# Attention scores of even and odd heads queued in pairs, in turn, in two PSUM banks

## The chip, the cores and the metric

The kernel runs on one core of one Trainium2 chip. The metric is the device time of one execution in microseconds. The engines are TensorE (PE in the rows; PEld is its weight loads), VectorE (DVE), ScalarE (ACT), GpSimd (POOL) and the DMA queues, which SyncE (SP) and others issue. Each engine works through its own queue in order and waits for others by semaphores.

## What is computed

Two transformer blocks over 256 tokens of width 1024, all in fp32: a gated MLP layer and a sliding-window attention layer, then a second block with a neighbourhood attention, a dilated attention and a product-key expert layer. Only the three attentions matter here. Cut to that:

```python
# sliding window (16 heads of 64, keys shared by 8 heads, sink per head)
scores = einsum('bnqhrd,bnkhd->bnhrqk', q, k_band) * 64 ** -0.5
scores = where(mask, scores, -inf)
m = maximum(max(scores), sink); p = exp(scores - m)
o = einsum('bnhrqk,bnkhd->bnqhrd', p / (sum(p) + exp(sink - m)), v_band)

# neighbourhood (8 heads) and dilated (8 heads): a bias or a mask per key, softmax over the keys
s = einsum('bhqd,bhqkd->bhqk', q, k[idx]) * 64 ** -0.5 + bias
o = einsum('bhqk,bhqkd->bhqd', softmax(s), v[idx])
```

The kernel computes each of them over all 256 keys (or 128 for the first token tile of the sliding window), with tables that add a large number where a key is out of reach.

## The kernel before, in words

Each projection is a product of three passes (`mm3`, lines 295 to 297): weights are split into a high and a low part, `hi` by ScalarE (L115, or L121 where the weights are scaled) and `lo` by VectorE or GpSimd (L116, L122), out of raw buffers that SyncE's DMA queue fills ahead. A projection goes in pieces: a unit of weights, its matmuls, then `tick()`. A tick runs what was deferred to it, and after that some units of a background list `bg`, as many as a rate says (3.0 in block B, 3.25 and 6.0 in block C). The scheduler is manual: every engine's queue has the order in which the program is written, and the ticks thus set where attention stands between the projections.

`attn` (L566) fills that list. Its work is cut into items. An item is one token tile of 128 queries and either four heads with 128 keys or two heads with 256 keys, and all heads of an item are even, or all are odd. A head has 64 dimensions; those of even heads lie in partitions 0 to 63 of `qT` and `kT`, or of `qkT`, and those of odd heads in 64 to 127. So the score products of an even item use one half of TensorE's rows, those of an odd item the other half. In the program's lists even and odd items alternate. An item has three units:

- S, `score(i)`: one PSUM tile `tr` (a bank) with the score products (L584); then for each head VectorE adds the bias and takes the minimum of the negated scores (L589, into `sc` and `nm`), and ScalarE takes the exponential with its sum (L592, into `pe`).
- T, `tr(i)`: four transposes of `pe` by TensorE (L608) into a `tr` tile, which ScalarE (L613, even items) or VectorE (L611, odd items) copies to `pT`.
- O, `ov(i)`: eight records of products of `pT` with v (L626) into the tile `o`. After the last item of eight heads `o_evac` follows on VectorE. In block C it divides (`yo`, L883), takes a sum of squares on ScalarE, a power on GpSimd (L212) and scales `yo` on VectorE (L888).

The order of the units was S(i), T(i-2), O(i-3), over and over. There are three `tr` banks. Others use them too: transposes of q (L696, copied by ScalarE at L697), of y and of other activations (L250, evacuated to `yThi` by ScalarE and to `yTlo` by VectorE, L252, L253, L258, L259), products for a bias table `nab` (L823, read by VectorE at L825) and two products for the modulation (`ada`, L451, read at L455). For the modulation VectorE also adds up `ada_acc` (L425) from weights that GpSimd's DMA queue loads.

Block B (sliding window) has 12 items. Block C has two times 8: the neighbourhood heads, here C0, and the dilated heads, here C1.

Of the kernel before, what the change touches and what calls it, by code (L numbers as in the profile page):

```python
# [37 lines left out]
P = 128  # L38
# [12 lines left out]
class Model:  # L51
# [514 lines left out]
    def attn(self, pool, items, qT, kT, v, bias, sink, osink, ready=lambda: True):  # L566


        nc = self.nc
        st = {}  # L570

        def score(i):
            tt, heads, kt = items[i]
            nk = len(kt) * P
            ps = self.tr_tile()
            pe = pool.tile([P, 512], F32, name="pe", tag="pe", bufs=3)
            key = "sum", tt, heads[0] // 8
            if key not in st:
                st[key] = pool.tile([P, 2, 8], F32, name="den", tag="den", bufs=3)
                st["min", key] = self.SM.tile([P, 8], F32, name="nm", tag="nm", bufs=3), []  # L580
            sm, (nm, seen) = st[key], st["min", key]
            for j, hd in enumerate(heads):
                js = slice(j * nk, (j + 1) * nk)
                nc.tensor.matmul(ps[:, js], qT(hd)[:, tt * P:(tt + 1) * P], kT(hd)[:, kt[0] * P:kt[0] * P + nk],  # L584
                                 start=True, stop=True)
            for j, hd in enumerate(heads):
                js = slice(j * nk, (j + 1) * nk)
                s = pool.tile([P, nk], F32, name="sc", tag="sc", bufs=4)
                nc.vector.tensor_tensor_reduce(s, ps[:, js], bias(hd, tt), scale=1.0,  # L589
                                               scalar=sink[:, hd:hd + 1] if sink is not None else BIG,  # L590
                                               op0=OP.add, op1=OP.min, accum_out=nm[:, hd % 8:hd % 8 + 1])
                nc.scalar.activation(pe[:, js], s, AF.Exp, scale=-1.0, bias=nm[:, hd % 8:hd % 8 + 1],  # L592
                                     accum_out=sm[:, 0, hd % 8:hd % 8 + 1])
                seen.append(hd)
            if sink is not None and len(seen) == 8:
                g0 = heads[0] // 8 * 8
                nc.vector.tensor_tensor(sm[:, 1], nm, sink[:, g0:g0 + 8], op=OP.subtract)
                nc.scalar.activation(sm[:, 1], sm[:, 1], AF.Exp)
            st[i] = pe

        def tr(i):
            tt, heads, kt = items[i]
            n = len(kt)
            ps = self.tr_tile()
            pe = st.pop(i)
            m = len(heads) * n
            for q in range(m):
                nc.tensor.transpose(ps[:, q * P:(q + 1) * P], pe[:, q * P:(q + 1) * P], self.ident)  # L608
            pT = pool.tile([P, 512], F32, name="pT", tag="pT", bufs=2)
            if i % 2:  # L610
                nc.vector.tensor_copy(pT[:, :m * P], ps[:, :m * P])  # L611
            else:
                nc.scalar.activation(pT[:, :m * P], ps[:, :m * P], AF.Copy)  # L613
            st[i] = pT

        def ov(i):
            tt, heads, kt = items[i]
            pT = st.pop(i)
            grp = heads[0] // 8
            if ("o", tt, grp) not in st:  # L620
                st["o", tt, grp] = self.o_tile()
            o = st["o", tt, grp]
            for j, hd in enumerate(heads):
                for q, kk in enumerate(kt):
                    c = j * len(kt) + q
                    nc.tensor.matmul(o[:, (hd % 8) * 64:(hd % 8 + 1) * 64], pT[:, c * P:(c + 1) * P], v(hd, kk),  # L626
                                     start=q == 0, stop=q == len(kt) - 1)
            if heads[-1] % 8 == 7:
                osink(tt, grp, st.pop(("o", tt, grp)), st.pop(("sum", tt, grp)))

        n = len(items)
        for i in range(n + 3):
            if i < n:
                self.bg.append(lambda i=i: score(i))
            if 0 <= i - 2 < n:
                self.bg.append(lambda i=i: tr(i - 2))
            if 0 <= i - 3 < n:
                self.bg.append(lambda i=i: ov(i - 3) if ready() else False)


    def block_b(self):
# [700 lines left out]
```

## Time and profile before

| | us |
|---|---|
| three runs | 1334.18, 1329.62, 1328.78 (median 1329.62) |
| the profiled execution | 1334.21 |
| its span, first to last instruction | 1332.5 |
| TensorE busy | 1292.4 (97%) |
| VectorE busy | 1006.7 (76%) |
| ScalarE busy | 643.7 (48%) |

A row of the views in order of time gives the start, the duration, the engine, the line, the operation, the tiles written and read, the shape and, in brackets, how long the engine had been idle before it and what ended that. Neighbours of one kind are merged (x8). TensorE's matmuls overlap in the pipeline, so a group's end and the next one's start lie over each other: what a group costs is read from its start to the next group's start. An fp32 product is two records. The granted clock (PEclk) is a share of 2.4 GHz, so 0.50 is 1.2 GHz.

### The profile page before, as it was taken

How to read it: one execution, taken by the hardware profiler on the slowest of the kernel's cores; microseconds unless marked ns; L12 is line 12 of the kernel's file. 1: busy time of each engine (PE TensorE's matmuls, PEld its weight loads, DVE VectorE, ACT ScalarE, POOL GpSimd, SP SyncE). 2: the span in 40 equal slices, each digit the busy share in tenths (PEclk: the TensorE clock that was granted, in tenths of full speed). 3: DMA queues.
4: the chain of work that ended last, by engine and by line, in shares of the span. 5: the costliest groups of instructions: out<-in, count | busy, mean ns of one | idle time of the engine just before them, and what ended most of it. 6: DMA issues, size and time to landing. Idle time of an engine off the chain costs nothing.

```text
span 1332.5 us, 21495 instructions
## 1 busy us (share of the span) xinstructions
PE 1292.4 (97%) x7898; PEld 1146.2 (86%) x7898; DVE 1006.7 (76%) x2086; ACT 643.7 (48%) x1125; POOL 158.5 (12%) x149
## 2 busy tenths in 40 slices
PE   8999999998999989999999999999999999999997
PEld 6888777786987869999999999999988888888886
DVE  5789777757756577979999999999765668666565
ACT  5555355663545335544544444444455555445544
POOL 1111112014102134730000000000000001000001
PEclk9999999998989989999999999999999999999999
DMA  7988787523765334555554444444457668655552
GB/s 275 336 266 278 235 267 217 141 80 126 258 232 182 118 122 151 172 170 169 180 168 162 140 143 143 143 143 143 159 188 238 224 213 272 205 192 190 194 196 100
DMA packets 85417, 250.90 MB, mean 188 GB/s; under 512 B 7776, under 2 KB 8944, under 8 KB 84672
## 3 DMA queue, kind: packets, MB, share of 16 engines
q1 hardware_dynamic: 74240, 208.17, 46.5%
q0 software_dynamic: 10208, 39.63, 9.3%
q10 hardware_dynamic: 864, 1.73, 0.3%
q8 instruction: 62, 1.02, 0.3%
q14 instruction: 43, 0.35, 0.1%
HBM read 247.40 MB, written 2.10 MB: 187 GB/s over the span
## 4 chain that ended last, share of the span: by engine, by line
PE 77%; DVE 11%; DMA 4%; issue 4%; ACT 2%; POOL 1%; POOLq 0%; ACTq 0%; DVEq 0%
PE mm L297 22%; PE mm L295 22%; PE mm L296 22%; PE tr L1092 4%; DVE lo L116 4%; DMA ada<-in_ada_w 2%; PE o L626 1%; PE tr L584 1%; DMA raw<-in_a_w_out 1%; DVE G L1047 1%; DVE G L1045 1%; PE tr L608 1%; POOL lo L116 1%; DMA ada<-in_norm_g 1%; ACT pe L592 1%
## 5 line engine op out<-in xcount | busy, mean ns | idle before, releaser
L116 DVE TENSOR_TENSOR lo<-raw,hi 128x1024 fp32r<-128x1024 f32 x340 | 416.5, 1229 | 131.7 <-ACT hi L115 129.3
L115 ACT ACTIVATE hi<-raw 128x1024 fp32r<-128x1024 f32 x376 | 394.5, 1052 | 182.7 <-PE mm L296 72.3
L295 PE MATMUL mm<-hThi,hi 128*128 128x256 f32 x1248 | 360.2, 289 | 0.0
L297 PE MATMUL mm<-hThi,lo 128*128 128x256 f32 x1248 | 354.3, 284 | 3.7 <-DVE lo L116 3.5
L296 PE MATMUL mm<-hTlo,hi 128*128 128x256 f32 x1248 | 353.3, 283 | 0.0
L297 PEld LDWEIGHTS mm<-hThi,lo 128*128 128x128 f32 x1248 | 239.4, 192 | 5.6 <-DVE lo L116 5.5
L295 PEld LDWEIGHTS mm<-hThi,hi 128*128 128x128 f32 x1248 | 239.7, 192 | 0.4 <-issue 0.3
L296 PEld LDWEIGHTS mm<-hTlo,hi 128*128 128x128 f32 x1248 | 239.9, 192 | 0.1
L296 PE MATMUL mm<-lo,whi 128*128 128x512 f32 x512 | 199.2, 389 | 0.0
L295 PE MATMUL mm<-hi,whi 128*128 128x512 f32 x512 | 199.2, 389 | 0.0
L297 PE MATMUL mm<-hi,wlo 128*128 128x512 f32 x512 | 199.2, 389 | 0.0
L1152 ACT ACTIVATE whi<-G 128x256 fp32r<-128x256 f32 x128 | 53.4, 418 | 167.1 <-PE mm L296 166.6
L295 PE MATMUL mm<-hi,hThi 128*128 128x512 f32 (+1 forms) x320 | 129.3, 404 | 0.7 <-ACT hThi L278 0.3
L296 PE MATMUL mm<-lo,hThi 128*128 128x512 f32 (+1 forms) x320 | 126.1, 394 | 0.5 <-DVE lo L116 0.5
L297 PE MATMUL mm<-hi,hTlo 128*128 128x512 f32 (+1 forms) x320 | 126.3, 395 | 0.2 <-DVE hTlo L279 0.2
L296 PEld LDWEIGHTS mm<-lo,whi 128*128 128x128 f32 x512 | 96.1, 188 | 20.1
L295 PEld LDWEIGHTS mm<-hi,whi 128*128 128x128 f32 x512 | 96.1, 188 | 20.1
L297 PEld LDWEIGHTS mm<-hi,wlo 128*128 128x128 f32 x512 | 96.1, 188 | 19.7
L1153 DVE TENSOR_TENSOR wlo<-G,whi 128x256 fp32r<-128x256 f32 x128 | 55.7, 436 | 62.2 <-ACT whi L1152 62.2
L116 POOL TENSOR_TENSOR lo<-raw,hi 128x1024 fp32r<-128x1024 f32 x36 | 89.1, 2480 | 104.8 <-ACT hi L115 104.8
L1084 DVE TENSOR_SCALAR ohg<-iota,slotT 128x128 f32<-128x128 f32 x256 | 87.4, 341 | 0.0
L1100 ACT ACTIVATE G<-tr 128x292 f32<-128x292 f32 (+31 forms) x64 | 19.7, 308 | 140.1 <-DVE G L1098 90.6
(239 smaller groups left out, 1627.4 us busy)
## 6 DMA issues: line engine op xcount, KB each, us to landing
raw<-in_u SPq DMA_DIRECT2D x128, 512.0 KB, 3.7
raw<-in_v SPq DMA_DIRECT2D x128, 512.0 KB, 4.4
raw<-in_a_w_in SPq DMA_DIRECT2D x48, 512.0 KB, 5.6
ada<-in_ada_w POOLq DMA_DIRECT2D x40, 512.0 KB, 4.9
raw<-in_w_in SPq DMA_DIRECT2D x24, 512.0 KB, 4.8
raw<-in_a_w_out SPq DMA_DIRECT2D x16, 512.0 KB, 5.9
raw<-in_b_w_in SPq DMA_DIRECT2D x16, 512.0 KB, 5.3
raw<-in_wq SPq DMA_DIRECT2D x12, 512.0 KB, 3.6
```

Of the source, the lines that this page charges most:

```text
L115: nc.scalar.activation(hi, raw, AF.Copy)
L116: e.tensor_tensor(lo, raw, hi.bitcast(F32), op=OP.subtract)
L295: nc.tensor.matmul(out, l[0], r[0], start=start, stop=False, skip_group_check=shared)
L296: nc.tensor.matmul(out, l[0], r[1], start=False, stop=False, skip_group_check=shared)
L297: nc.tensor.matmul(out, l[1], r[0], start=False, stop=stop, skip_group_check=shared)
L584: nc.tensor.matmul(ps[:, js], qT(hd)[:, tt * P:(tt + 1) * P], kT(hd)[:, kt[0] * P:kt[0] * P + nk], start=True, stop=True)
L592: nc.scalar.activation(pe[:, js], s, AF.Exp, scale=-1.0, bias=nm[:, hd % 8:hd % 8 + 1], accum_out=sm[:, 0, hd % 8:hd % 8 + 1])
L1084: nc.vector.tensor_scalar(og[:, j], self.iota, slotT[:, 0, t:t + 1], slotT[:, 2, t:t + 1], op0=OP.is_equal, op1=OP.mult)
L1092: nc.tensor.matmul(ps[:, j * P:(j + 1) * P], o[:, j], og[:, j], start=True, stop=True)
L1100: nc.scalar.activation(G[:, nb:, t0:t0 + 4], src[:, nb:], AF.Copy)
L1152: nc.scalar.activation(hi, G[:, b], AF.Copy)
L1153: nc.vector.tensor_tensor(lo, G[:, b], hi.bitcast(F32), op=OP.subtract)
```

## The change

The products of items i and i+1 (even and odd) are queued together when S(i) runs, with one tile each, head by head in turn; S(i+1) then has only its VectorE and ScalarE part. The list is built in pairs: S(i), T(i-2), S(i+1), T(i-1), O(i-2), O(i-1). The number of units is the same. All further lines move by 12 to 14.

```diff
--- before.py
+++ after.py
@@ -566,23 +566,35 @@
     def attn(self, pool, items, qT, kT, v, bias, sink, osink, ready=lambda: True):
 
 
+
         nc = self.nc
         st = {}
+
+        def products(i):
+            pair = (i, i + 1)
+            for q in pair:
+                st["ps", q] = self.tr_tile()
+            tt, heads, kt = items[i]
+            nk = len(kt) * P
+            assert items[i + 1][0] == tt and items[i + 1][2] == kt and len(items[i + 1][1]) == len(heads)
+            for j in range(len(heads)):
+                for q in pair:
+                    hd = items[q][1][j]
+                    nc.tensor.matmul(st["ps", q][:, j * nk:(j + 1) * nk], qT(hd)[:, tt * P:(tt + 1) * P],
+                                     kT(hd)[:, kt[0] * P:kt[0] * P + nk], start=True, stop=True)
 
         def score(i):
             tt, heads, kt = items[i]
             nk = len(kt) * P
-            ps = self.tr_tile()
+            if i % 2 == 0:
+                products(i)
+            ps = st.pop(("ps", i))
             pe = pool.tile([P, 512], F32, name="pe", tag="pe", bufs=3)
             key = "sum", tt, heads[0] // 8
             if key not in st:
                 st[key] = pool.tile([P, 2, 8], F32, name="den", tag="den", bufs=3)
                 st["min", key] = self.SM.tile([P, 8], F32, name="nm", tag="nm", bufs=3), []
             sm, (nm, seen) = st[key], st["min", key]
-            for j, hd in enumerate(heads):
-                js = slice(j * nk, (j + 1) * nk)
-                nc.tensor.matmul(ps[:, js], qT(hd)[:, tt * P:(tt + 1) * P], kT(hd)[:, kt[0] * P:kt[0] * P + nk],
-                                 start=True, stop=True)
             for j, hd in enumerate(heads):
                 js = slice(j * nk, (j + 1) * nk)
                 s = pool.tile([P, nk], F32, name="sc", tag="sc", bufs=4)
@@ -629,13 +641,15 @@
                 osink(tt, grp, st.pop(("o", tt, grp)), st.pop(("sum", tt, grp)))
 
         n = len(items)
-        for i in range(n + 3):
-            if i < n:
-                self.bg.append(lambda i=i: score(i))
-            if 0 <= i - 2 < n:
-                self.bg.append(lambda i=i: tr(i - 2))
-            if 0 <= i - 3 < n:
-                self.bg.append(lambda i=i: ov(i - 3) if ready() else False)
+        for i in range(0, n + 2, 2):
+            for j in (0, 1):
+                if i < n:
+                    self.bg.append(lambda i=i + j: score(i))
+                if i >= 2:
+                    self.bg.append(lambda i=i + j: tr(i - 2))
+            for j in (0, 1):
+                if i >= 2:
+                    self.bg.append(lambda i=i + j: ov(i - 2) if ready() else False)
 
 
     def block_b(self):
```

`products` takes two `tr` tiles at once. Which bank a tile gets is settled when the program is built: at the start of a stretch the second pair's odd tile gets the bank of the very first tile (in C0 tr_3229 that of tr_3206), and waits until VectorE's L589 steps on it are done. The first T after a pair's S takes the third bank. In C1's dense part the last T (into tr_3915) takes the bank of item 6 (tr_3888).

TensorE's queue at the start of C0, before; S are L584, T are L608, and tr_3206, tr_3218 and tr_3228 are the tiles of items 0 to 2, tr_3278 that of item 3:

```order
L584 MATMUL tr_3206<-qkT_2903 128x256 x2
L584 MATMUL tr_3218<-qkT_2903 128x256 x2
L584 MATMUL tr_3228<-qkT_2903 128x256 x2
...
L608 MATMUL tr_3271<-ident_92,pe_3207 128x128 x4
L584 MATMUL tr_3278<-qkT_2903 128x256 x2
L608 MATMUL tr_3288<-ident_92,pe_3219 128x128 x4
```

The same place now; S are L583, T are L620, and tr_3206, tr_3207, tr_3228, tr_3229 are the tiles of items 0 to 3:

```order
L583 MATMUL tr_3206<-qkT_2903 128x256
L583 MATMUL tr_3207<-qkT_2903 128x256
L583 MATMUL tr_3206<-qkT_2903 128x256
L583 MATMUL tr_3207<-qkT_2903 128x256
L583 MATMUL tr_3228<-qkT_2903 128x256
L583 MATMUL tr_3229<-qkT_2903 128x256
L583 MATMUL tr_3228<-qkT_2903 128x256
L583 MATMUL tr_3229<-qkT_2903 128x256
...
L620 MATMUL tr_3274<-ident_92,pe_3212 128x128 x4
L620 MATMUL tr_3288<-ident_92,pe_3221 128x128 x4
```

Left out are 24 projection matmuls. Item 3's products moved from behind them, and from behind the first T, to ahead of them.

TensorE's queue in C1's dense part, before; O are L626, and items 4 to 7 have their scores in tr_3830, tr_3853, tr_3874 and tr_3905:

```order
L626 MATMUL o_3825<-vs_2904,pT_3742 128x64 x4
L584 MATMUL tr_3830<-qkT_2903 128x256 x2
L608 MATMUL tr_3842<-ident_92,pe_3689 128x128 x4
L626 MATMUL o_3825<-vs_2904,pT_3759 128x64 x4
L584 MATMUL tr_3853<-qkT_2903 128x256 x2
L608 MATMUL tr_3863<-ident_92,pe_3745 128x128 x4
L626 MATMUL o_3825<-vs_2904,pT_3847 128x64 x4
L584 MATMUL tr_3874<-qkT_2903 128x256 x2
L608 MATMUL tr_3884<-ident_92,pe_3831 128x128 x4
L626 MATMUL o_3825<-vs_2904,pT_3868 128x64 x4
L584 MATMUL tr_3905<-qkT_2903 128x256 x2
L608 MATMUL tr_3915<-ident_92,pe_3854 128x128 x4
```

Now, the second half of it (the first half is the same with items 0, 1, 4, 5, 2 and 3); O are L638:

```order
L638 MATMUL o_3825<-vs_2904,pT_3854 128x64 x4
L638 MATMUL o_3825<-vs_2904,pT_3868 128x64 x4
L583 MATMUL tr_3888<-qkT_2903 128x256
L583 MATMUL tr_3889<-qkT_2903 128x256
L583 MATMUL tr_3888<-qkT_2903 128x256
L583 MATMUL tr_3889<-qkT_2903 128x256
L620 MATMUL tr_3901<-ident_92,pe_3840 128x128 x4
L620 MATMUL tr_3915<-ident_92,pe_3856 128x128 x4
```

Two O, two S and two T now follow each other, where O, S and T took turns. On VectorE, item 6's L589 stood ahead of the evacuation of `yo` before:

```order
L589 ISA sc_3878,nm_3833<-tr_3874,dib_2902 128x256
...
L589 ISA sc_3881,nm_3833<-tr_3874,dib_2902 128x256
...
L883 TENSOR_TENSOR yo_2907<-o_3825,den_3668 128x512
L888 TENSOR_SCALAR yo_2907<-yo_2907,rs_r_3902 128x512
```

Now it stands behind it (L601 was L589, L897 and L902 were L883 and L888):

```order
L897 TENSOR_TENSOR yo_2907<-o_3825,den_3673 128x512
L902 TENSOR_SCALAR yo_2907<-yo_2907,rs_r_3885 128x512
L601 ISA sc_3895,nm_3842<-tr_3888,dib_2902 128x256
...
L601 ISA sc_3898,nm_3842<-tr_3888,dib_2902 128x256
```

Since O(3) ends the first eight heads, and it is now written ahead of S(6), VectorE reads item 6's scores only after `yo` is scaled.

## Rows read from the trace of the kernel before

**Rows 1.** First part of the page: busy us, share of the span, instructions.

```profile
PE 1292.4 (97%) x7898; PEld 1146.2 (86%) x7898; DVE 1006.7 (76%) x2086; ACT 643.7 (48%) x1125; POOL 158.5 (12%) x149
```

**Rows 2.** TensorE in order of time (start, us, instruction), a lone S in C0.

```profile
386.45 1.00 PE L626 MATMUL o<-vs,pT 128*128 128x64 f32 x8
387.38 1.13 PE L584 MATMUL tr<-qkT 64*128 64x256 f32 x4
388.44 0.66 PE L608 MATMUL tr<-ident,pe 128*128 128x128 f32 x4
...
395.99 1.00 PE L626 MATMUL o<-vs,pT 128*128 128x64 f32 x8
396.81 0.36 PE L295 MATMUL mm<-hThi,hi 128*128 128x256 f32 x1
```

**Rows 3.** TensorE in order of time, the three S that open C0.

```profile
371.06 1.99 PE L584 MATMUL tr<-qkT 64*128 64x256 f32 x12
372.98 0.39 PE L295 MATMUL mm<-hThi,hi 128*128 128x256 f32 x1
```

**Rows 4.** TensorE and VectorE in order of time, the start of block B.

```profile
238.19 0.50 PE L295 MATMUL mm<-hi,hThi 128*128 128x512 f32 x1
238.43 0.08 DVE L589 DVE_READ_ACCUMULATOR2_ANT nm<- 128x1 f32 x1
```

**Rows 5.** ScalarE and TensorE in order of time, block B, the second T.

```profile
243.13 0.57 ACT L613 ACTIVATE pT<-tr 128x512 f32<-128x512 f32 x1
243.76 0.66 PE L608 MATMUL tr<-ident,pe 128*128 128x128 f32 x4 [0.20 <-ACT pT L613]
```

**Rows 6.** ScalarE, TensorE and VectorE in order of time, block B, transposes of q.

```profile
256.62 1.06 ACT L697 ACTIVATE qT<-tr 128x512 f32<-128x512 f32 x2
257.25 0.66 PE L608 MATMUL tr<-ident,pe 128*128 128x128 f32 x4 [0.41 <-ACT qT L697]
257.96 0.69 DVE L722 TENSOR_TENSOR q<-o,den 128x512 f32<-128x512 f32 x1
```

**Rows 7.** TensorE, VectorE and ScalarE in order of time, block B, transposes of y.

```profile
285.00 1.04 PE L250 MATMUL tr<-ident,q 128*128 128x128 f32 x8
285.20 0.69 DVE L825 TENSOR_TENSOR nab<-nam,tr 128x512 f32<-128x512 f32 x1 [1.31 <-PE tr L823]
285.64 1.09 ACT L252 ACTIVATE yThi<-tr 128x512 fp32r<-128x512 f32 x2 [0.67 <-PE tr L250]
286.27 1.29 DVE L253 TENSOR_TENSOR yTlo<-tr,yThi 128x512 fp32r<-128x512 f32 x2 [0.38 <-ACT yThi L252]
```

**Rows 8.** VectorE in order of time, the start of C0.

```profile
373.73 1.28 DVE L425 SCALAR_TENSOR_TENSOR ada_acc<-ada,silu_c,ada_acc 128x1024 f32<-128x1024 f32 x1 [7.41 <-DMA ada<-in_ada_w]
...
377.89 0.08 DVE L589 DVE_READ_ACCUMULATOR2_ANT nm<- 128x1 f32 x1
```

**Rows 9.** TensorE in order of time, the first T of C0.

```profile
378.31 1.18 PE L608 MATMUL tr<-ident,pe 128*128 128x128 f32 x4 [2.21 <-DVE nm L589]
```

**Rows 10.** Stretches: length, busy us of PE, PEld, DVE, ACT, POOL; PEclk, DMA share, GB/s.

```profile
378.31:385.14 6.83, 6.83 (x26) 5.46 (x27) 5.67 (x15) 5.62 (x17) 0.53 (x1) 0.50 0.76 259
...
429.51:432.93 3.42, 3.42 (x11) 2.42 (x11) 2.03 (x7) 2.60 (x7) 0.23 (x1) 0.50 0.70 214
```

**Rows 11.** TensorE and VectorE in order of time, the start of C1.

```profile
421.70 0.50 PE L295 MATMUL mm<-hi,hThi 128*128 128x512 f32 x1
423.00 0.09 DVE L589 DVE_READ_ACCUMULATOR2_ANT nm<- 128x1 f32 x1
428.83 1.38 PE L584 MATMUL tr<-qkT 64*128 64x256 f32 x4 [2.76 <-DVE yTlo L259]
```

**Rows 12.** TensorE and VectorE in order of time, the dense part of C1.

```profile
448.50 1.13 PE L584 MATMUL tr<-qkT 64*128 64x256 f32 x4
451.01 0.49 DVE L888 TENSOR_SCALAR yo<-yo,rs_r 128x512 f32<-128x512 f32 x1 [1.71 <-POOL rs_r L212]
452.10 0.69 DVE L611 COPY pT<-tr 128x512 f32<-128x512 f32 x1
```

## The prediction

> **What bounds the kernel now.** I read the page's first part, then the chain that ended last, then TensorE's order of time in the three stretches in which attention runs. TensorE is busy for 97% of the span [rows 1], and the chain runs over it nearly everywhere, so a microsecond taken off TensorE there is a microsecond of the kernel, unless a wait takes its place. The stretches are 236 to 304 us (block B), 371 to 417 us (block C, neighbourhood heads: C0) and 419.8 to 459 us (block C, dilated heads: C1). An item is one score step with its transposes and its product with v. I call its three units S, T and O. A unit is queued between pieces of a projection, so a lone S costs its products and two changes between 64 and 128 rows. In [rows 2] O takes 0.93 us up to the S, and S 1.06 us up to the T; where a projection follows O instead, O takes 0.81. So a lone S costs 1.06 + 0.12 = 1.18 us.
>
> Where an even and an odd S already stand next to each other, they share the array. Each of the three stretches starts with three S in a row, and in C0 their twelve records take 371.06 to 372.98 = 1.92 us [rows 3], about two lone ones, for three items. So the overlap is real on this chip before the change, and the alternate order inside a pair is not what brings it: standing next to each other is. The Trainium skill says otherwise on this point ("TensorE: Matmul & The Clock Gate", Part 3, The mechanism): matmuls start and end in program order. By that the three clusters would gain about another 0.6 us each from the alternation, 2 us in all; the row decides against it, and the sum has no such term.
>
> **What it saves.** Block B has 12 items, C0 and C1 have 8 each; less the three of the clusters, 9, 5 and 5 S stand alone. In each stretch the first joins the opening cluster, where its row half is free, and the rest form pairs: 4 pairs for 8 in B, 2 for 4 in C0 and C1. That takes away 5 + 3 + 3 = 11 lone S, 5.9 + 3.5 + 3.5 = 12.98 us.
>
> **What it makes wait.** A pair holds two of the three `tr` banks from its first product until DVE has read both tiles, and its T and O units now stand T T and O O. The built program names for each wait what ends it; the durations are those of the rows.
>
> *Block B.* (a) The second pair's odd tile takes the bank of the very first tile, which DVE leaves at 238.51 [rows 4]. The cluster would otherwise have ended near 238.19, as now; it goes on from 238.55 for a lone S, 1.06, to 239.6: +1.4. (b) The second T stands right behind the first, in the bank that ScalarE empties with a 0.57 us copy [rows 5]: 0.8 with the ways there, where 0.45 is waited today (0.20 of it before the T at 243.76, the rest in the S ahead of it): +0.35. (c) The transposes of q (L696) take the third bank and one of the pair's, and both T behind them wait for ScalarE's copies of q. Today one T does, 0.41, with the copies ending near 257.2 [rows 6]. Item 4's score step on DVE moves behind the evacuation of o (0.69 us, 1.1 with its two small steps [rows 6]), and ScalarE's exponentials, two splits and copies follow it: the copies end near 257.7 and 258.2. I count 2.5 us of waits against 1.2: +1.3. (d) A T now waits until DVE has read a nab product (0.69 us [rows 7]) out of the bank that it takes, less the T ahead of it: +0.5. (e) Where y is transposed (L250), the third bank is late by 0.5, the next T waits for the yThi and yTlo chain of the bank that it takes (285.64 to 286.9, T ready at 285.88 + 0.5), and the second T for the copy of the first: 0.5 + 0.6 + 0.8 = 1.9 [rows 7]. Sum of B: -5.9 + 1.4 + 0.35 + 1.3 + 0.5 + 1.9 = -0.45 us.
>
> *C0.* The fourth tile again takes the first one's bank. DVE stood idle 7.4 us here for the ada weights, then did ada_acc and two splits, and left that bank only at 377.97 [rows 8]. TensorE reaches the product at 372.0 and cannot pass it: behind it are the rest of the pair and 24 projection matmuls, that run in this time today. The cluster then ends at 378.02 + 1.06 = 379.1 and not at 372.98: +6.1. The wait of 2.21 at 378.31 [rows 9] falls away: -2.2. The clock: today it is at 1.2 GHz from 378.31 to 385.14 [rows 10], right after that wait, which costs half of 6.83. A wait of 5.5 us will bring it down too. I take 5.1 us at the low level, between the two lengths that the rows show (3.42 and 6.83): -0.85, bounds -1.7 and 0. Small waits around the ada product (its two banks, then ScalarE's copy): +0.6. Sum: -3.5 + 6.1 - 2.2 - 0.85 + 0.6 = +0.15.
>
> *C1.* The first bank is left at 423.09 [rows 11], so the cluster ends at 424.2 and not at 421.70: +2.5. The 2.76 us wait of the fourth S on yTlo [rows 11] falls away with 0.3 behind it: -3.05. But the first T now takes that bank and waits for the same chain, which starts later (about 1.75), and the second T waits for ScalarE's copy behind that chain (0.95): +2.7. Then comes the densest part, four items with no projection between them, which run without a wait today. O O S S T T O O S S T T: the second T waits 0.55 for DVE's score step, the next O 0.85 for ScalarE's copy, which comes behind the exponentials. The last T needs the bank of item 6, whose score step stands on DVE behind the scaling of yo. That scaling waits for the square sum and GpSimd's power: from the end of O at 448.50 to the end of that score step today it is 3.6 us (452.10) [rows 12]. TensorE needs 1.06 + 0.41 and a change for S S and T, so 2.2 us are waited. Together +3.6. The clock: one low stretch of 3.42 today [rows 10]; two gaps near 2 us now: +0.85, bounds 0 and +3.4. Sum: -3.5 + 2.5 - 3.05 + 2.7 + 3.6 + 0.85 = +3.1.
>
> Total: -0.45 + 0.15 + 3.1 = +2.8 us. DVE, ScalarE and the DMA queues do the same work as before. What hides the pairs' DVE and ScalarE steps elsewhere is 2.8 us of projection behind each; where there is none, the waits above are what it costs.
>
> **Rivals.** A: the waits are shorter than I read them, or hidden by work that moves up, and the 11 lone S come off whole: -13.0, about 1317 us. Half of it would be 1323. For it: TensorE bounds, and the overlap is seen. Against: the opening clusters' waits hang on DVE times that do not depend on TensorE (238.51, 377.97, 423.09), 6 to 8 us of the price by themselves. The Trainium skill stands on this side: "TensorEngine Tiling (Array Packing)", Theoretical Speedup, gives up to twice the speed for a contraction of at most 64. For the products themselves the trace agrees [rows 3].
>
> B, the slower side: the clock. Today each wait over 2 us in block C is followed by a stretch at 1.2 GHz [rows 9 to 11]. If the two gaps at the start of C1 give two such stretches, the 3.6 us of waits in the dense part another, and C0's lasts 6.83, that is +1.7, +1.7 to 3.4 and +0.85 on top: 1337 to 1338 us. It decides once the dense part loses its clock.
>
> C: the pairs do not overlap as queued. A pair then costs some 2.1 - 0.2 = 1.9 us, each cluster of four twice its length: the saving shrinks to about 3 us and the clusters add 4.5, near 1346 us. The cluster speaks against it [rows 3].
>
> **How the numbers follow.** The profiled execution took 1334.21 us (span 1332.5), 4.6 above the median of 1329.62; I add the sum to either: 1337.0 profiled, and 1332.4 as the median. Forecast 0.62 (its own range 1327 to 1336, by the clock's bounds, -1.7 and +2.5, and two to three microseconds of the small waits), A 0.08, B 0.25, C 0.05. A measurement can tell about 0.5%, 6.65 us: below 1323.0 is faster, above 1336.3 slower. So faster 0.08, same 0.62, slower 0.30. The range of 1326 to 1340 leaves out A and C.
>
> **What would show it.** Right: the score records fall from 22 groups to 11, with a pair taking 1.1 us; TensorE stands still once in each opening cluster, longest (5 to 6 us) in C0, waiting for DVE's score step; in the dense part the last T waits some 2 us for a score step that follows GpSimd. Wrong: an opening cluster without a wait, pairs of 1.9 us, or block B shorter by more than 3 us.

## The result, and the profile after

Four executions of the changed kernel took 1345.45 to 1348.01 us (median 1346.41), four of the kernel before 1328.78 to 1335.58 (median 1331.9). The ratio is 1.0115, 95% interval 1.0092 to 1.0138: slower by some 15 us, where 2.8 were forecast and 1340 us was the upper end of the range. The profiled execution took 1345.52 us (span 1343.8).

The page's first part, answering to [rows 1], shows TensorE 5 us less busy, in a span 11.3 us longer:

```profile
PE 1287.4 (96%) x7898; PEld 1140.9 (85%) x7898; DVE 1012.7 (75%) x2086; ACT 644.3 (48%) x1125; POOL 158.1 (12%) x149
```

The next view gives stretches: length, busy us of PE, PEld, DVE, ACT, POOL; granted clock, DMA share, GB/s. The three rows are block B, C0 and C1, cut at the same projection matmuls in every kernel (records 850 to 1060, 1340 to 1530 and 1530 to 1640). The kernel before:

```profile
221.57:311.23 89.66, 87.98 (x472) 69.48 (x471) 60.83 (x153) 49.16 (x116) 11.70 (x6) 1.00 0.44 129
367.61:414.45 46.84, 44.63 (x309) 39.55 (x308) 28.47 (x57) 22.39 (x51) 4.56 (x9) 0.93 0.63 214
414.45:468.49 54.04, 50.76 (x277) 40.83 (x275) 32.43 (x69) 25.05 (x61) 10.29 (x13) 0.97 0.44 143
```

The changed kernel:

```profile
223.76:320.34 96.58, 86.46 (x473) 68.02 (x472) 63.33 (x153) 49.55 (x116) 11.68 (x6) 0.96 0.42 123
376.71:420.96 44.25, 40.65 (x308) 36.57 (x307) 28.54 (x57) 22.43 (x51) 4.56 (x9) 0.96 0.64 215
420.97:480.24 59.27, 52.67 (x277) 41.12 (x275) 34.26 (x69) 25.14 (x61) 9.98 (x13) 0.91 0.41 137
```

Length less busy time is what TensorE waits: 1.7, 2.2 and 3.3 us before, 10.1, 3.6 and 6.6 after. Block B is 6.9 us longer and C1 5.2, C0 2.6 shorter. These are lengths of one execution each; how far a stretch moves between executions of one kernel is shown further below. Another 2.2 us of difference between the two traces arise before attention begins (221.57 against 223.76).

The pairs do what they should. TensorE in order of time, the changed kernel, a pair in block B:

```profile
277.69 1.13 PE L583 MATMUL tr<-kT,qT 64*128 64x256 f32 x8
278.76 0.50 PE L295 MATMUL mm<-hi,hThi 128*128 128x512 f32 x1
```

That is 1.07 us for two items, where a lone S takes 1.06 [rows 2]. There are 11 groups of score records now, 22 before. In each opening cluster TensorE stands and waits for VectorE's score step, as forecast (B, C0 and C1, in order of time):

```profile
240.78 1.13 PE L583 MATMUL tr<-kT,qT 64*128 64x256 f32 x6 [0.95 <-DVE nm L601]
```

```profile
384.99 1.85 PE L583 MATMUL tr<-qkT 64*128 64x256 f32 x6 [3.27 <-DVE nm L601]
```

```profile
429.60 2.07 PE L583 MATMUL tr<-qkT 64*128 64x256 f32 x6 [1.74 <-DVE nm L601]
```

What was not forecast in this size is the place in block B where y is transposed. It answers to [rows 7]; all engines in order of time, rows of other work left out:

```profile
277.28 2.37 POOL L116 TENSOR_TENSOR lo<-raw,hi 128x1024 fp32r<-128x1024 f32 x1 [23.70 <-ACT hi L115]
...
278.60 2.13 DVE L746 TENSOR_TENSOR q<-q,sgb 128x1024 f32<-128x1024 f32 x1
...
280.65 0.47 DVE L601 CUSTOM_DVE_ANT_0 sc<-tr,mask,b_sinks 128x256 f32<-128x256 f32 x1
...
281.21 1.28 ACT L604 ACT_TABLE_LOAD   x1 [4.01 <-DVE nm L601]
...
281.63 1.02 PE L837 MATMUL tr<-rev,flip 128*128 128x512 f32 x2
...
282.49 0.60 PE L250 MATMUL tr<-ident,q 128*128 128x128 f32 x4
...
283.50 1.04 ACT L115 ACTIVATE hi<-raw 128x1024 fp32r<-128x1024 f32 x1
284.45 0.57 ACT L252 ACTIVATE yThi<-tr 128x512 fp32r<-128x512 f32 x1
284.57 1.22 DVE L116 TENSOR_TENSOR lo<-raw,hi 128x1024 fp32r<-128x1024 f32 x1 [3.04 <-ACT hi L115]
285.72 0.68 DVE L839 TENSOR_TENSOR nab<-nam,tr 128x512 f32<-128x512 f32 x1
286.31 0.68 DVE L253 TENSOR_TENSOR yTlo<-tr,yThi 128x512 fp32r<-128x512 f32 x1
286.45 1.12 PE L250 MATMUL tr<-ident,q 128*128 128x128 f32 x4 [3.36 <-DVE nab L839]
...
287.36 1.06 PE L620 MATMUL tr<-ident,pe 128*128 128x128 f32 x4
...
289.17 1.11 PE L620 MATMUL tr<-ident,pe 128*128 128x128 f32 x4 [0.75 <-ACT pT L625]
...
289.94 0.77 PE L295 MATMUL mm<-hi,hThi 128*128 128x512 f32 x1
...
294.24 1.02 PE L837 MATMUL tr<-rev,flip 128*128 128x512 f32 x2
```

It is read from the wait of 3.36 us upwards. The transposes of y (L250) wait for the read of nab, which stands on VectorE behind a weight split (`lo`). That waits 3.04 us for ScalarE's `hi`, which comes behind the exponentials and a table load, and these wait for VectorE's score step, behind the gating of y (L746). In the new list S(8) follows O(4) and O(5) at once, so all of it falls into one projection piece. In the kernel before the table load came 10 us ahead of the transposes (274.45), the split just before them was GpSimd's, and VectorE read nab at once.

### The profile page after: what moved, and what is told of

Its sections match the earlier page's. It is cut to its first block, busy times and chain, and to the rows that moved or that the text cites. A ratio compares the mean times of both kernels' runs of the same rounds, so it can differ in the third digit from the quotient of the medians.

```text
span 1343.8 us, 21494 instructions
## 1 busy us (share of the span) xinstructions
PE 1287.4 (96%) x7898; PEld 1140.9 (85%) x7898; DVE 1012.7 (75%) x2086; ACT 644.3 (48%) x1125; POOL 158.1 (12%) x149
## 3 DMA queue, kind: packets, MB, share of 16 engines
q10 hardware_dynamic: 864, 1.73, 0.4%
## 4 chain that ended last, share of the span: by engine, by line
PE 70%; DVE 13%; DMA 6%; issue 5%; ACT 4%; POOL 1%; ACTq 0%; POOLq 0%; DVEq 0%
PE mm L295 20%; PE mm L297 20%; PE mm L296 20%; DVE lo L116 5%; PE tr L1106 4%; DMA raw<-in_a_w_in 3%; DMA ada<-in_ada_w 2%; PE o L638 1%; ACT hi L115 1%; DMA raw<-in_a_w_out 1%; DVE G L1059 1%; DVE G L1061 1%; POOL lo L116 1%; PE tr L583 1%; ACT pe L604 1%
## 5 line engine op out<-in xcount | busy, mean ns | idle before, releaser
L1166 ACT ACTIVATE whi<-G 128x256 fp32r<-128x256 f32 x128 | 53.4, 418 | 167.0 <-PE mm L296 165.2
```

The costliest lines, as they stand in the source:

```text
L1166: nc.scalar.activation(hi, G[:, b], AF.Copy)
```

## The experiments

For each kernel TensorE's time in the three stretches is split in the same way: its waits; what 1.2 GHz costs (half of its busy time there); and the rest, its work at full clock. The table is worked out from all TensorE records and the granted clock. These columns are of one execution, whose whole time stands under "traced". The median of all executions and the ratio to the kernel before (95% interval) stand beside it; neighbouring runs were measured against the same executions of the kernel before, whose median was 1330.5 to 1331.9. Where the traced time lies far from the median (e2, e7 and e14), the columns say less about the typical execution.

| kernel | B + C0 + C1, us | waits | 1.2 GHz | work | traced us | median us | ratio |
|---|---|---|---|---|---|---|---|
| before | 190.5 | 7.2 | 5.1 | 178.3 | 1334.21 | 1331.9 | |
| b2_before (again) | 189.4 | 7.2 | 3.4 | 178.8 | 1332.96 | one run, 1332.96 | |
| changed | 200.1 | 20.3 | 9.8 | 170.0 | 1345.52 | 1346.41 | 1.0115 (1.0092 to 1.0138) |
| e1_no_turns | 201.4 | 21.7 | 7.5 | 172.2 | 1344.82 | 1344.77 | 1.0105 (1.0083 to 1.0127) |
| e2_list_only | 204.6 | 12.8 | 13.0 | 178.8 | 1350.47 | 1344.23 | 1.0092 (1.0067 to 1.0117) |
| e3_pairs_only | 190.9 | 15.6 | 6.8 | 168.4 | 1334.20 | 1335.38 | 1.0026 (1.0009 to 1.0043) |
| e4_lo_gpsimd | 196.3 | 20.7 | 5.1 | 170.4 | 1338.70 | 1340.35 | 1.0079 (1.0054 to 1.0103) |
| e5_pairs_late | 191.3 | 13.2 | 7.8 | 170.3 | 1337.95 | 1337.93 | 1.0052 (1.0032 to 1.0071) |
| e6_pairs_C0 | 187.0 | 6.9 | 3.4 | 176.7 | 1332.11 | 1330.95 | 0.9993 (0.9978 to 1.0008) |
| e7_changed_late | 201.2 | 20.6 | 9.7 | 170.9 | 1351.88 | 1346.81 | 1.0117 (1.0089 to 1.0145) |
| e15_changed_nab57 | 198.7 | 22.1 | 6.8 | 169.9 | 1344.29 | 1344.18 | 1.0098 (1.0081 to 1.0116) |
| e14_four_pairs | 181.0 | 6.2 | 0.0 | 174.8 | 1324.86 | 1327.7 | 0.9975 (0.9960 to 0.9991) |

In these two traces the change takes 8.3 us of work off TensorE and adds 13.1 of waits and 4.7 at the low clock.

**The two halves of the change, apart.** The first kernel below keeps the pairs and gives up the turns (both products of the even item E ahead of those of the odd item O: E E O O); the second keeps the list and gives up the pairs; the third keeps the pairs on the list of the kernel before.

```diff
 # e1_no_turns, in products()
-            for j in range(len(heads)):
-                for q in pair:
+            for q in pair:
+                for j in range(len(heads)):
 # e2_list_only, in products() and score()
-            pair = (i, i + 1)
+            pair = (i,)
-            if i % 2 == 0:
-                products(i)
+            products(i)
 # e3_pairs_only: the end of attn as in the kernel before
+        for i in range(n + 3):
+            S(i), T(i - 2), O(i - 3)
```

> The changed kernel (1346.4 us) with one difference: inside a pair the two products of the even head's tile stand first and those of the odd head's tile behind them, not in turn. Theory 1 (standing next to each other is what makes even and odd items share the array, and the loss comes from waits of the new list): a pair still takes 1.1 us and the time stays at 1346, within 3 us. Theory 2 (the alternation is what makes them share the array): a pair takes 1.9 to 2.1 us and the time goes to 1355 or more. Theory 3 (two row halves that write two banks in turn are themselves what costs): the time falls below 1340.

> The changed list (S T S T O O), but every S queues only its own products when it runs, so there are no pairs and no tile is held early. Theory 1 (the list is what costs: two T in a row, two O in a row, and VectorE's score steps behind the evacuation of o): slower than the kernel before by its waits without the opening clusters' (about 8 us), 1335 to 1342; and, since no S pairs up, the 13 us of lone S stay. Theory 2 (holding two of three banks from the first product on is what costs, and the list does nothing): 1332, as before.

> The pairs of the change, but with the list of the kernel before (S T O, over and over; every second S has no products of its own). Theory 1 (the list is what costs): the 11 lone S come off (-13.0 us), the opening clusters still wait (about +1.4, +3.3 and +1.7), a T still waits now and then for a score step: faster than before, 1320 to 1328. Theory 2 (the banks that a pair holds are what costs): 1340 to 1346, like the changed kernel.

The turns are worth nothing in the total: the intervals of e1 and of the changed kernel lie over each other, and its pairs of two products take 1.07 us too. Only pairs with four products of 128 columns each are longer; the one that stands alone takes 1.64 us against 1.09. Both kinds in e1:

```profile
276.36 1.14 PE L583 MATMUL tr<-kT,qT 64*128 64x256 f32 x8
277.43 0.50 PE L295 MATMUL mm<-hi,hThi 128*128 128x512 f32 x1
```

```profile
264.07 1.71 PE L583 MATMUL tr<-kT,qT 64*128 64x128 f32 x16
265.71 0.50 PE L295 MATMUL mm<-hi,hThi 128*128 128x512 f32 x1
```

The list alone costs 12 us (e2), more than Theory 1 gave it. Its work is that of the kernel before, and the chain at the transposes of y is there without any pair:

```profile
289.43 1.23 DVE L116 TENSOR_TENSOR lo<-raw,hi 128x1024 fp32r<-128x1024 f32 x1 [3.04 <-ACT hi L115]
290.57 0.68 DVE L837 TENSOR_TENSOR nab<-nam,tr 128x512 f32<-128x512 f32 x1
...
291.31 1.11 PE L618 MATMUL tr<-ident,pe 128*128 128x128 f32 x4 [3.25 <-DVE nab L837]
```

The pairs alone (e3) don't bring their 10 us of work either: Theory 1 said 1320 to 1328, Theory 2 1340 to 1346, and the median of 1335.4 lies between them. Waits grow by 8.5 us. The largest in block B is a T whose bank is a nab tile that VectorE reads only behind the rotation of q and a weight split; before, that T had another bank and TensorE went on for a piece:

```profile
253.69 0.66 PE L620 MATMUL tr<-ident,pe 128*128 128x128 f32 x4 [2.65 <-DVE nab L837]
```

So neither theory is right by itself: list and pairs each have a price. By the ratios the two add up: 12.2 us (e2) and 3.5 (e3) against 15.3 of the changed kernel, each known to some 3 us. At the transposes of y the wait comes with the list alone: the 24 projection matmuls around that place (records 972 to 996, though not the same attention units stand between them) take 13.1 us in the kernel before, 12.8 in e3, 19.6 in e2 and 19.2 in the changed kernel.

**The place at the transposes of y.** Three kernels take one link of the chain away. e4 lets GpSimd compute that one `lo`; the others move the nab products (by one piece; by one piece and the second four by one more).

```diff
 # e4_lo_gpsimd
-    ENG_BO, ... = (10, 10), ...
+    ENG_BO, ... = (8, 10), ...
 # e10_changed_flip7: FLIP = 7;  e15_changed_nab57: FLIP = 7 and
-                self.defer(self.FLIP + 6 * t + g, ...put(t, g))
+                self.defer(self.FLIP + 5 * t + g, ...put(t, g))
```

> The changed kernel, but the low part of one weight unit of block B's second projection (the lo at 284.57 us that VectorE computes ahead of the nab read) is computed by GpSimd. In the changed kernel VectorE waits 3.04 us at that lo for ScalarE's hi, behind the exponentials, the nab read stands behind it, and TensorE's transposes of y wait 3.36 us for that read. Theory 1 (that queue order is the cost of the place): the nab read ends near 283.5, the wait of 3.36 falls to 1 us or less, the low clock stretch behind it (6.83 us) may go too: 1341 to 1344. Theory 2 (the bank is late whatever VectorE does ahead): no change, 1346.

> The changed kernel (1346.4 us) with the nab products one piece earlier, so that none stands ahead of the transposes of y at 282 us, where TensorE waited 3.36 us for VectorE's nab read and then ran 6.83 us at 1.2 GHz. Moving one weight split off VectorE there (e4_lo_gpsimd) brought 6 us. Theory 1 (the place is one queue: bank, nab read, weight split, exponentials): again 4 to 7 us come off, 1339 to 1343. Theory 2 (what helped was the weight split alone, the nab bank is not needed for it): 1345 to 1347.

> The changed kernel (1346.4 us) with the nab products moved so that the last one stands a whole piece ahead of the transposes of y and none beside them; in e10_changed_flip7 and e13_changed_nab one still stood there, and the 3.36 us wait with it. Theory 1 (the bank of nab is the cause): the transposes do not wait, the T behind them at most 1 us, 1338 to 1342. Theory 2 (the weight split that VectorE has ahead, waiting for ScalarE's exponentials and hi, holds up yTlo just as it held up nab): the transposes do not wait, but the T behind them waits 3 to 4 us for yTlo, 1343 to 1346.

e4 brought 6.1 us by the medians (4.8 by the ratios). Nab is read at once, and the transposes wait 0.34 us. The T behind them then waits 1.73 for yTlo:

```profile
281.69 0.69 DVE L839 TENSOR_TENSOR nab<-nam,tr 128x512 f32<-128x512 f32 x1 [1.14 <-PE tr L837]
...
282.43 0.66 PE L250 MATMUL tr<-ident,q 128*128 128x128 f32 x4 [0.34 <-DVE nab L839]
...
284.82 1.31 PE L620 MATMUL tr<-ident,pe 128*128 128x128 f32 x8 [1.73 <-DVE yTlo L253]
```

Not all of the gain lies at this place. The same 24 projection matmuls, the changed kernel and then e4:

```profile
278.76:297.99 19.23, 15.12 (x71) 11.62 (x69) 9.05 (x18) 7.03 (x14) 3.26 (x2) 0.82 0.24 82
```

```profile
277.75:294.00 16.25, 14.17 (x70) 10.62 (x68) 7.93 (x17) 6.81 (x14) 5.65 (x3) 0.89 0.30 97
```

They are 3.0 us shorter: 2.0 of waits, and 3.41 us at 1.2 GHz behind them in place of 6.83. The other 3.8 us between the two traces lie mostly before attention, in C0 and in C1, which this edit does not touch, less 1.6 that e4 lost elsewhere in block B.

e10 (1344.72 us, 1.0084, 1.0063 to 1.0105) told nothing on this: only the last nab product left its place, another still stood at the transposes, and the wait was 3.36 again. e15 moved it away, and what Theory 2 said of the waits held. The eight transposes run without a wait (285.73), and the T waits 3.77 us for yTlo, behind the same split:

```profile
285.73 1.03 PE L250 MATMUL tr<-ident,q 128*128 128x128 f32 x8
...
288.66 1.23 DVE L116 TENSOR_TENSOR lo<-raw,hi 128x1024 fp32r<-128x1024 f32 x1 [3.04 <-ACT hi L115]
289.81 1.28 DVE L253 TENSOR_TENSOR yTlo<-tr,yThi 128x512 fp32r<-128x512 f32 x2
...
290.54 1.22 PE L620 MATMUL tr<-ident,pe 128*128 128x128 f32 x7 [3.77 <-DVE yTlo L253]
```

So the wait goes with the split on VectorE that waits for ScalarE, and not with the bank of nab: 4.1 us in the changed kernel (3.36 and 0.75), 3.77 in e15, 2.1 in e4. What holds the T up in e4 for the last 1.73 us no run takes away. The time of e15 alone would not tell the theories apart, since the moved nab product meets a new wait of 2.41 us in block B (at 259.78; the trace names nothing that ended it).

**The opening clusters and nab, with the pairs.** An empty unit behind S(1) puts the second pair one piece later: on the old list (e5), in C0 alone (e6) and on the changed list (e7). e8 and e9 move nab by one piece without and with pairs, e11 to e13 by more.

```diff
         for i in range(n + 3):
+            if i == 2:
+                self.bg.append(lambda: None)
```

> Pairs on the list of the kernel before, as in e3_pairs_only (1335.4 us), and one empty unit behind the second S, so that the first tick of each stretch queues one pair and the second pair comes a projection piece later, when its fourth bank is nearly free. Theory 1 (the opening clusters eat the gain of the pairs: waits of 0.95, 3.24 and 1.80 us in e3_pairs_only, and a stretch at 1.2 GHz behind two of them, 1.7 us each): of these 9.4 us some 6 to 8 come off, the rest comes back as a wait on the same score step a little later; 1327 to 1330. Theory 2 (VectorE's and ScalarE's steps set the pace of attention, so that whatever TensorE saves is waited at the next bank): the same waits elsewhere, 1333 to 1337.

> The kernel before in block B and in C1; only in C0 pairs on the list of the kernel before with the empty unit. In e3_pairs_only C0 alone was 3.65 us shorter than before (43.19 against 46.84), the only stretch that gained. Theory 1 (stretches add up): 3 to 5 us faster than before, 1326 to 1329. Theory 2 (what C0 gains is waited later, for transfers or at C1's start): 1331, as before.

> The changed kernel (1346.4 us) with the same empty unit behind its second S; every other unit keeps its order, but the ticks now cut the list elsewhere: pair 2 comes one projection piece later, and the two T of a pair stand in different pieces. Theory 1 (opening clusters and T T in a row are what costs in the changed list): 1335 to 1341. Theory 2 (the two banks that a pair holds and VectorE's queue cost the same wherever the cuts lie): 1344 to 1348.

> Pairs on the list of the kernel before (e3_pairs_only, 1335.4 us), with the nab products one piece earlier. There the longest wait of block B is 2.65 us, at a T whose bank holds a nab product that VectorE reads only after the rotation of q, with a stretch at 1.2 GHz behind it (3.41 us, 1.7 lost). Theory 1 (with two of three banks in a pair, the user of the third one decides, and nab is the late one): the wait and the stretch go, 4.4 us: 1330 to 1332. Theory 2 (VectorE's rotation of q itself sets the pace, so that the next user of a bank waits as long): 1334 to 1336.

None was faster than the kernel before. e5 lost the wait of B's cluster and all but 0.5 us of C0's, and got others at the next banks (1.76 and 2.72 us for nab in B, 2.48 for yTlo in C1). e7 changed nothing in the time. In its trace the waits in the 24 projection matmuls at the transposes of y are 1.6 us in place of 4.1, but an O of block B waits 3.96 us for VectorE's copy of pT, and the block is as long as in the changed kernel (96.8 us): what one wait gave back, another took. e6 can't be told from the kernel before (0.9993, 0.9978 to 1.0008). e9 lost the 2.65 us wait in its trace (block B 89.5 us), yet its median of eleven was 1335.61 (1.0022, 1.0009 to 1.0036). e9's traced execution (1331.56) was its second fastest. e8, the control without pairs, was 1332.41 (0.9997, 0.9985 to 1.0010), as expected. e11 to e13 missed what was expected of them, the control too: they moved the first nab product ahead of the data that it needs: TensorE waited 5.5 us in the control e12 (1340.15), 3.6 in e11 (1339.22), and 1.8 in e13 (1348.65) for transfers, and they tell nothing on pairs.

> The kernel before once more, for a second trace: how much of the 11.3 us between the two traces (of which 2.2 us lie before attention starts, at 221 us) is chance of one execution. Expected: 1329 to 1335, block B's stretch (records 850 to 1060 of the projections) 89.7 us within 0.5, C0's and C1's 46.8 and 54.0 within 1.7, one half of a stretch at 1.2 GHz.

The second trace of the kernel before shows what one trace is worth. Both block B (93.16 us, not 89.66) and C0 (41.87, not 46.84) miss what was expected:

```profile
222.03:315.19 93.16, 89.58 (x473) 70.61 (x472) 61.02 (x153) 49.03 (x116) 11.71 (x6) 0.98 0.46 128
371.57:413.44 41.87, 41.73 (x309) 37.21 (x307) 28.19 (x57) 22.38 (x51) 4.56 (x9) 1.00 0.70 234
```

In block B the difference is a wait ahead of attention's first products, for ScalarE's copy of q, with a stretch of 3.41 us at 1.2 GHz behind it. ScalarE had stood 6.87 us for weights from DMA until 229.23 (4.52 in the first trace). In the first trace that wait is 0.74 us, and e6, with block B as in the kernel before, takes 89.67 us. The row of b2:

```profile
234.17 0.66 PE L696 MATMUL tr<-ident,q 128*128 128x128 f32 x4 [2.65 <-ACT qT L697]
```

With the same code in C0, three more traces have 41.8 (e8), 42.0 (e16) and 43.6 (e12). VectorE's `ada_acc` (L425), which waits for the ada weights, starts 3.9 to 4.1 us into the stretch in b2, e8 and e16, and the first T waits 0.2 us at most; it starts at 5.8 us in e12 (a wait of 1.84) and at 6.1 in the first trace. So the wait of 2.21 us at C0's first T [rows 9] belonged to an execution in which the ada weights came late, and so did the stretch at 1.2 GHz behind it [rows 10]. Against 41.9 us the C0 of e3 (43.19) is no gain at all, and that of e6 (41.01) is one of 0.9 us, which is why e6 fell short.

**Pairs only where no bank is late.** In e3 one piece of block B had gained without any wait: records 936 to 984, items 6 to 9, 21.22 us against 23.63 (both lengths come back to 0.01 us: 23.63 in b2 and e6, 21.22 in e14 and e16). e14 joins only those two pairs and two in C0, on the old list; e16 only the two in B.

```diff
-            pair = (i, i + 1)
+            pair = (i, i + 1) if i in paired else (i,)
 # paired: (6, 8) in block B, (4, 6) in C0, none in C1
```

> The kernel before with only four of its twenty-eight items' pairs joined: items 6 and 7, 8 and 9 of block B, 4 and 5, 6 and 7 of C0, on the list of the kernel before. In e3_pairs_only the stretch of block B with those two pairs (records 936 to 984 of the projections) took 21.22 us against 23.63, with no wait; C0's two took 2.6 us off the work and gave up to 1.9 back in waits. Theory 1 (a pair gains 1.1 us where the third bank comes free in time and nothing stands on VectorE ahead of its reads): 2.4 + 0.7 to 2.3 = 3 to 4.7 us faster than before, 1327 to 1329. Theory 2 (what is gained there is waited for at the next place, the transposes of y or C1's start): 1331 to 1332.

> The same with block B's two pairs only. Theory 1: 2.4 us faster than before, 1329 to 1330. Theory 2: 1331 to 1332.

e14 is faster than both kernels, as Theory 1 said: 1327.7 us, ratio 0.9975 (0.9960 to 0.9991). The gain is smaller than the spread of its single executions (1323.75 to 1331.42). The piece of block B in the kernel before and in e14:

```profile
257.66:281.29 23.63, 23.63 (x129) 18.85 (x128) 13.40 (x42) 14.85 (x39) 2.39 (x1) 1.00 0.31 103
```

```profile
258.32:279.54 21.22, 21.22 (x130) 17.10 (x128) 12.07 (x38) 14.84 (x39) 2.39 (x1) 1.00 0.34 108
```

No wait in either, 2.41 us for two pairs. At the end of B 0.95 us are given back, 0.64 of it as a wait for VectorE's gating of y. C0 is 39.40 us, 2.5 under the 41.87 of the second trace, without a wait. By the traces that makes 3.9 us, by the medians 2.8. e16 is 2.0 us below in the median, and its interval reaches over no change (0.9994, 0.9979 to 1.0008).

## Why the prediction was wrong, point by point

*The saving* was right in kind: 11 groups fewer, pairs of 1.07 us, overlap by standing next to each other. Of the 12.98 us, 8.3 left TensorE's work, 9.9 in e3; the clusters' terms had already given some 3 us of it back. That the turns inside a pair bring nothing, as the sum had it, e1 shows. The Trainium skill's two-fold figure ("TensorEngine Tiling (Array Packing)", Theoretical Speedup) agrees with the pairs, 1.07 us for two against 1.06 for one.

*Block B* was forecast at -0.45 us and came out at +6.9. Here the prediction failed most. The cluster is right (3.60 us from 238.24 against 2.16: +1.4). The second T too (0.69 of wait), and the transposes of q (+1.4: 0.31 and 1.83 of wait). The step that failed is term (e), the transposes of y: 1.9 us forecast. The transposes took 4.87 us instead of 0.87, the two T 2.57 instead of 0.79, the twelve matmuls behind them 4.31 instead of 2.86, partly at 1.2 GHz: 7.2 us. I had taken the nab read from [rows 7], where VectorE does it at once, and had not followed VectorE's queue in the new order up to the weight split and to the engine that it waits for. e2, with the list and no pair, has this wait; e3, with pairs and the old list, has not; e4, which moves that split, gets 3.0 us back at this place.

*C0* was forecast at +0.15 and is -2.6 against its own trace, but +2.4 against 41.87. The failing step is "The wait of 2.21 at 378.31 [rows 9] falls away: -2.2", with the clock's -0.85 behind it: that wait was chance, as the second trace shows, and there was nothing to win. The wait in the cluster was 3.27 us, not 5.5. It follows the ada weights: `ada_acc` starts 0.5 us behind the cluster's start now (380.69 against 380.16), 2.7 us behind it in [rows 8] and [rows 3]. In e4, the changed kernel and e10 it starts 3.4, 4.0 and 4.3 us into the stretch, and the cluster waits 2.68, 3.27 and 3.61.

*C1* was forecast at +3.1 and is +5.2 in the first two traces. The waits are near the forecast: 1.74 in the cluster, 1.77 and 0.75 at the first two T. In the dense part the second T waits 0.37, the next O 0.60 and the last T 0.77; in e4, e13 and e15, where TensorE stayed at full clock there, the last one waits 2.11 us behind the scaling of yo, as forecast (2.2), here in e4:

```profile
453.56 0.48 DVE L902 TENSOR_SCALAR yo<-yo,rs_r 128x512 f32<-128x512 f32 x1 [1.72 <-POOL rs_r L212]
453.96 0.42 DVE L601 CUSTOM_DVE_ANT_0 sc<-tr,dib 128x256 f32<-128x256 f32 x1
...
454.88 0.63 PE L620 MATMUL tr<-ident,pe 128*128 128x128 f32 x4 [2.11 <-DVE nm L601]
```

What went beyond the forecast in that trace is the clock: 3.42 us at 1.2 GHz before [rows 10], 10.25 now, in two stretches:

```profile
429.62:436.45 6.83, 6.83 (x17) 4.95 (x18) 2.59 (x9) 3.73 (x13) 2.88 (x2) 0.50 0.41 147
456.93:460.35 3.42, 3.42 (x16) 2.34 (x15) 1.05 (x2) 0.72 (x2) 1.13 (x3) 0.50 0.00 0
```

That costs 3.4 us more, but part of it is chance of this execution. With the same code in C1, e4, e13 and e15 have one stretch of 3.41 us and a C1 of 57.4, and e10 takes 60.0. The C1 of the kernel before takes 53.4 to 56.4 us in eight traces (before, b2, e6, e8, e11, e12, e14 and e16). Between the middle values, 57.4 and 55.0, lie 2.5 us, between the means 3.4: the forecast of 3.1 agrees with that. The same wait of 2.76 us for yTlo [rows 11] has a stretch at 1.2 GHz behind it in the first trace, and none in e8 and e14.

*The rivals.* A (hidden waits) and C (no overlap) are excluded by the rows. That the median lies at 1346 us, which is C's number, is accident: C had pairs of 1.9 us. B, the clock, came true in part: 4.7 us over the three stretches of the first two traces, 2.9 of it in block B, where the prediction had none. Of the 11.7 us between the forecast of +2.8 and the 14.5 between the medians, block B makes 7.3 (5.3 of them in (e)) and C0 2.2. The rest, some 2 us, is not attributed, and neither are 2 of block B's.

What stays open: why e9 and e3 have the same median though e9's trace has lost the largest wait. Their executions spread over 3 to 6 us, and one trace of each does not tell. Open too is how far VectorE's and ScalarE's steps set the pace wherever a pair saves time, as e5 and e7 suggest; in the pieces of e14 they did not.

## What to carry to other kernels

In this kernel, packing two half-height products was worth its full microsecond where the second PSUM bank was free anyway (e14), and not elsewhere (e3). The new order of the units, which came along with the pairs, cost more than they did (12 us against 3.5), so measure the two apart. With three banks for many users, price each user of the remaining one by the queue of the engine that empties it, followed back to whatever that engine waits for in the new order, not by the duration of the read. And take a wait that a change is to remove from more than one trace before it is counted as a gain.

## What the runs showed of the hardware that was not expected

VectorE's product of 128x1024 (L746) took 2.13 us while GpSimd ran its split (277.28 to 279.65), where the same product took 1.22 us in the kernel before (281.26), with GpSimd idle. That is 0.9 us at the head of the chain above. The two ran side by side for 1.05 us, so the product stood nearly still meanwhile; in e4 it took 2.15 us and in e2 2.45, beside the same split. The Trainium skill ("GPSIMD Engine Reference", 1. Specifications) says that GpSimd shares its SBUF interfaces with VectorE and that VectorE's instructions with two SBUF inputs contend; these rows agree. And overlap reaches some way down TensorE's queue: with an item's products queued ahead of its partner's (e1) the two halves still share the array as fully as in turn when an item has two products (1.07 us), and less when it has four (1.64 against 1.09).
